# A modulation chunk's gate: products on VectorE in the feed-forward part instead of matmuls in the mixing part

## The chip, the cores and the metric

The kernel runs on one core of one Trainium2 chip. The time is that of one launch in device microseconds; a time is the median of several launches. One more launch was recorded by the profiler.

## The reference, cut to what matters

Two layers on 256 tokens `x` and 256 context tokens `ctx` of width 1024, followed by a second network of two blocks that the change doesn't touch. Each of the two layers computes from one vector `c` (and one `c_ctx` for the context) six chunks of 1024 modulation values; the last chunk, number 5, is the gate of the feed-forward part, and it is used only where that part's result is added.

```python
s_lat, s_ctx = silu(c), silu(c_ctx)
mod   = s_lat @ w_mod[i] + b_mod[i]      # w_mod[i]: 1024 x 6144
mod_c = s_ctx @ w_mod[i] + b_mod[i]
sh1, sc1, g1, sh2, sc2, g2 = split(mod, 6)

def _ffn_sublayer(x, shift, scale, gate, p):
    h = rms_norm(x, p['g_pre_ffn']) * (1 + scale) + shift
    f = square(relu(h @ p['w_ff1'])) @ p['w_ff2']     # 1024 -> 4096 -> 1024
    return x + gate * rms_norm(f, p['g_post_ffn'])
```

## The kernel before

All is float32. Each matmul of the layers is three passes (`mm3`, L212): stationary and moving operand are split in a high and a low part, and high x high, high x low and low x high are added. A weight tile `raw` (512 KB, a ring of 5) is loaded by a DMA that SyncE issues; ScalarE copies it to the high part `wh` (L226), VectorE subtracts for the low part `wl` (L227), 128x512 at a time, ten buffers each. SyncE's queue is in order: a load that waits for a free `raw` holds back all loads behind it.

The modulation values of layer 0 are made in two ways. Chunks 0 and 1 come at the very start. Chunks 2 to 5 are two units of 2048 columns in the mixing part (`mod_units((0, 1), (0, 2))`): for each of eight steps over the 1024 inputs, two `raw` tiles with two column groups each are loaded, and four float32 matmuls of 32 rows x 512 columns (L303), each on its own 32 columns of the array, add into one PSUM tile `fl`. Four transposes (L310) and an addition (L314) end a unit.

The modulation values of layer 1 are made during the feed-forward part of layer 0, by `mod_sums` (L323 to L357): VectorE multiplies a `raw` tile by the token's value and adds it to an accumulator `q` (L340 for the first product, L342 for the others, 128x512 each), a matmul with ones sums over the partitions (L346, one for each accumulator, on 32 columns of the array each, into `fl`), then four transposes and an addition follow. One call of `step()` issues the products of one `raw` tile: four where two token kinds are wanted, two where one is.

The feed-forward part (`ffn`) goes in eight rounds `r_` of 512 hidden features: a first product with w_ff1 (four tiles of features), the square of its positive part (L947 to L950), a second product with w_ff2 that is added to `acc` (L966). In round 0 the first product goes in two halves of 256 columns, that of the tokens `X` and that of the context `CTX`, since the context's input `h2c` is made last (transposes L420, scaling L424 and split L226/L227, from `modulated`). `mod_gate` (L387 to L395) spreads the gate over the partitions: 8 transposes (L393) and two copies into `q` buffers for each token kind; before, this stands at the head of `ffn`, and its four `q` buffers (of eight) stay in use until the end of it.

The order of the instructions on each engine is not that of the source. A scheduler in the build orders them by priority and by its own estimate of when operands are there; on the chip each engine then works through its list in order. Buffers of a ring are handed out in that order, too.

Of the kernel before, what the change touches and what calls it, by code (L numbers as in the profile page):

```python
# [1 line left out]

# [62 lines left out]
def body(ctx, tc, A, out):  # L65
# [44 lines left out]
    def FL():  # L110
        return pfl.tile([P, 512], F32, tag="fl", name=nm("fl"))
# [208 lines left out]
    ones = C([P, 32], "c_ones")  # L320
    POOL.memset(ones, 1.0)

    def mod_sums(i):  # L323

        nrow = A["w_mod"][i].rearrange("(k p) n -> p k n", p=P)
        for kinds, nb, b0 in (((0, 1), 2, 0), ((0, 1), 2, 2), ((0,), 4, 4), ((0,), 4, 8)):
            accs = []
            for b in range(b0, b0 + nb):  # L330
                acc = [Q() for _ in kinds]
                accs += acc
                for k in range(0, KT, 2):
                    r = raw.tile([P, 1024], F32, tag="raw", name=nm("raw")).rearrange("p (k c) -> p k c", k=2)
                    SP.dma_start(r, nrow[:, k:k + 2, 512 * b:512 * b + 512])
                    for q in range(2):
                        for o, a in zip(kinds, acc):
                            w = sT[:, k + q, o:o + 1]
                            if k + q == 0:
                                DVE.tensor_scalar(a, r[:, q, :], w, None, ALU.mult)  # L340
                            else:
                                DVE.scalar_tensor_tensor(a, r[:, q, :], w, a, ALU.mult, ALU.add)  # L342
                    yield
            ps = FL()
            for g, a in enumerate(accs):
                PE.matmul(ps[32 * g:32 * g + 32, :], ones, a, start=True, stop=True, skip_group_check=True)  # L346
            r = R()
            ACT.copy(r, ps)
            for j in range(4):
                PE.transpose(ps[:, j * P:(j + 1) * P], r[:, j * P:(j + 1) * P], ident)  # L350
            nr = len(kinds)
            t4 = ps.rearrange("p (j b r q) -> p b j r q", j=4, b=nb, r=nr)
            for b in range(nb):
                k = 4 * (b0 + b)
                DVE.tensor_tensor(mods[i][:, k:k + 4, 0:nr], t4[:, b, :, :, 0],
                                  cols[i][:, O_BM + k:O_BM + k + 4, None].to_broadcast([P, 4, nr]), ALU.add)
            yield  # L357

    def mod_units(*units):

        def steps():
            for i, u in units:
                yield from mod_steps(i, [2048 * u + 512 * g for g in range(4)], 512, FL())
        return stepping(steps())

    def stepping(it):
# [536 lines left out]
    def ffn(i, h2, h2x, h2c, step, done):  # L903
        last = i == 1
        pairs = (X,) if last else (X, CTX)
        acc = {}
        gate = {r: mod_gate(i, 5, O_GQF, r) for r in ((0,) if last else (0, 1))}
        for r_ in range(8):
            if r_ == 0 and last:

                nb = 2
                Ws = [wblk(A["w_ff1"][i], [(512 * q, 512)], keep=KT if q else 0) for q in range(nb)]
                first = {(t, q): (U(F32R), U(F32R)) for t in range(2) for q in range(nb)}
                for t in range(2):
                    for q in range(nb):
                        ps = AN()
                        mm3(ps, tok(h2x, t, Ws[q]))
                        r, f2 = R(), R()
                        ACT.activation(r, ps, AF.Relu)
                        DVE.tensor_tensor(f2, r, r, ALU.mult)  # L920
                        tp = TP()
                        for ft in range(4):
                            PE.transpose(tp[:, ft * P:(ft + 1) * P], f2[:, ft * P:(ft + 1) * P], ident)
                        split(tp, *first[t, q])
            if last and r_ < nb:
                parts, srcs = (), ()
                fT = None
            else:
                W6 = wblk(A["w_ff1"][i], [(512 * r_, 512)])
                if last:  # L930
                    parts, srcs = ((0, 256),), (h2x,)
                elif r_ == 0:
                    parts, srcs = ((256, 512), (0, 256)), (h2x, h2c)
                else:
                    parts, srcs = ((0, 512),), (h2,)
                if last:
                    q_ = [U(F32R) for _ in range(4)]
                    fT = [(q[:, 0:256], q[:, 256:512]) for q in q_]
                else:
                    fT = [(U(F32R), U(F32R)) for ft in range(4)]  # L940
            for (a, b), src in zip(parts, srcs):
                for ft in range(4):
                    ps = AN()
                    mm3(ps[:, a:b], feat(W6, ft, src, 0, b - a))
                    r, f2 = R(), R()
                    h, l = cut(fT[ft], a, b)
                    ACT.activation(r[:, a:b], ps[:, a:b], AF.Relu)  # L947
                    ACT.activation(h, r[:, a:b], AF.Square)
                    POOL.tensor_tensor(f2[:, a:b], r[:, a:b], r[:, a:b], ALU.mult)  # L949
                    DVE.tensor_tensor(l, f2[:, a:b], f(h), ALU.subtract)  # L950
                    if r_:
                        step(2)
            W7 = [wblk(A["w_ff2"][i], [(512 * n, 512)], 4 * r_, 4) for n in range(2)]
            for pair in (pairs if r_ == 7 else (sum(pairs, ()),)):
                by_token = r_ == 7 and pair == X
                for t, n in [(t, n) for t in pair for n in range(2)] if by_token else [(t, n) for n in range(2) for t in pair]:
                    ps = AN()
                    if fT is None:
                        mm3(ps, [(cut(first[t - 2, r_], k * P, (k + 1) * P), W7[n][k]) for k in range(4)])
                    else:  # L960
                        mm3(ps, tok(fT, t - 2 if last else t, W7[n]))
                    if r_ == 0:
                        acc[t, n] = U()
                        ACT.copy(acc[t, n], ps)
                    else:
                        DVE.tensor_tensor(acc[t, n], acc[t, n], ps, ALU.add)  # L966
                    if r_ == 7 and n == 1:
                        postnorm(t, [acc[t, 0], acc[t, 1]], gate[0 if t >= 2 else 1])
                if r_ == 7:
                    done(pair)  # L970
# [333 lines left out]
    out_projection(0, yT, mid0)  # L1304
    sc1 = C([P, 8, 2], "c_scale1_1")
    POOL.memset(mods[1], 0.0)
    step = stepping(mod_sums(1))
    hT, hc, hx = both()

    def end0(pair):  # L1310
# [24 lines left out]
    def step(n=1):  # L1335
        calls[0] += 1
        if calls[0] == 20:
            first.append(ple(0))
# [31 lines left out]
```

## Time and profile before

| | us |
|---|---|
| median of 3 launches | 1543.09 |
| the three launches | 1543.09, 1537.67, 1543.42 |
| the profiled launch | 1537.98 |
| its span from the first to the last instruction | 1535.9 |
| TensorE (PE) busy in it | 1470.2 |
| VectorE (DVE) busy | 1036.4 |
| ScalarE (ACT) busy | 740.4 |
| GpSimd (POOL) busy | 308.2 |

The mixing part of layer 0 lies at about 55 to 325 us of the span, its feed-forward part at about 325 to 685 us, layer 1 behind it to about 1050 us. Round 0 of the feed-forward part ends on TensorE at 362.87 us. Times of single instructions overlap on TensorE: what one takes of the engine is read from its start to the start of the next.

### The profile page before, as it was taken

The page shows a single profiled execution, that of the slowest core. Times are in us where ns is not written, and L with a number is a line of the kernel's source. Part 1 is how long each engine was busy: PE and PEld are TensorE (multiplying, and loading weights), DVE is VectorE, ACT ScalarE, POOL GpSimd, SP SyncE. Part 2 cuts the span into 40 slices and gives each one's busy share as a digit, 9 for nine tenths or more (in the row PEclk, how much of TensorE's full clock was granted, in tenths as well). Part 3 has the DMA queues.
Part 4 walks back from the last instruction along what each step waited for, and adds up shares of the span by engine and source line. Part 5 has one row for each costly group of instructions (what it writes and reads, how often), then busy time and mean ns, then how long its engine had stood idle before and what let it go on. Part 6 is the DMA issues. An engine that isn't in the chain of part 4 may idle for free.

```text
span 1535.9 us, 23433 instructions
## 1 busy us (share of the span) xinstructions
PE 1470.2 (96%) x8417; PEld 1215.3 (79%) x8417; DVE 1036.4 (67%) x2057; ACT 740.4 (48%) x1594; POOL 308.2 (20%) x356
## 2 busy tenths in 40 slices
PE   6997999999999999998899899999999999999998
PEld 4766678888878888878797689997888889878886
DVE  3559556478597557478776756676876786567866
ACT  3433345564233333255556654565566457445663
POOL 1225201150001111034331301112310320021110
PEclk9998999999999999999999999999999999999999
DMA  9854622325366546334423546555436550645442
GB/s 294 266 182 153 219 84 88 97 66 195 123 219 206 180 152 200 109 83 135 132 76 117 165 139 213 188 195 169 153 107 203 162 179 15 219 139 180 138 149 69
DMA packets 131687, 236.51 MB, mean 154 GB/s; under 512 B 12624, under 2 KB 31251, under 8 KB 131571
## 3 DMA queue, kind: packets, MB, share of 16 engines
q1 hardware_dynamic: 130688, 233.46, 47.0%
q0 software_dynamic: 704, 1.50, 0.3%
q8 instruction: 66, 1.08, 0.3%
q14 instruction: 50, 0.41, 0.1%
q10 hardware_dynamic: 179, 0.06, 0.0%
HBM read 233.87 MB, written 1.11 MB: 153 GB/s over the span
## 4 chain that ended last, share of the span: by engine, by line
PE 84%; DVE 7%; DMA 4%; issue 2%; ACT 2%; POOL 1%; SPq 0%; ACTq 0%; DVEq 0%; POOLq 0%
PE sc L212 47%; PE mm L212 20%; PE tp L459 3%; DVE wl L227 2%; PE fl L303 2%; DMA raw<-in_w_mod_dram 1%; DMA raw<-in_ple_w_gate_dram 1%; PE fl L212 1%; DMA raw<-in_w_in_dram 1%; PE sc L793 1%; PE mm L639 1%; PE sc L1083 1%; PE sc L634 1%; DVE u L782 1%; PE sc L1108 1%
## 5 line engine op out<-in xcount | busy, mean ns | idle before, releaser
L227 DVE TENSOR_TENSOR wl<-raw,wh 128x512 fp32r<-128x512 f32 (+1 forms) x606 | 421.2, 731 | 141.1 <-ACT wh L226 138.1
L226 ACT CAST wh<-raw 128x512 fp32r<-128x512 f32 (+1 forms) x606 | 359.2, 620 | 307.0 <-PE sc L212 104.5
L212 PE MATMUL sc<-wh,u 128*128 128x512 f32 (+2 forms) x1424 | 458.6, 389 | 3.5 <-DVE r L505 2.0
L212 PEld LDWEIGHTS sc<-wh,u 128*128 128x128 f32 x1424 | 265.4, 189 | 58.8 <-ACT p L226 2.2
L212 PE MATMUL sc<-wl,u 128*128 128x512 f32 (+2 forms) x712 | 274.6, 387 | 0.1
L212 PE MATMUL sc<-u,wh 128*128 128x256 f32 (+1 forms) x1072 | 265.1, 336 | 1.8 <-ACT wh L226 1.1
L212 PE MATMUL mm<-wh,u 128*128 128x512 f32 (+1 forms) x648 | 219.3, 395 | 1.0 <-ACT u L226 1.0
L212 PEld LDWEIGHTS sc<-u,wh 128*128 128x128 f32 x1072 | 184.0, 191 | 24.5 <-issue 2.0
L212 PE MATMUL sc<-u,wl 128*128 128x256 f32 (+1 forms) x536 | 178.0, 335 | 0.0
L212 PEld LDWEIGHTS sc<-wl,u 128*128 128x128 f32 x712 | 134.6, 189 | 24.8 <-DVE wl L227 0.5
L949 POOL TENSOR_TENSOR r<-r 128x256 f32<-128x256 f32 (+1 forms) x60 | 64.3, 1073 | 420.1 <-ACT r L947 380.2
L212 PEld LDWEIGHTS mm<-wh,u 128*128 128x128 f32 x648 | 122.2, 190 | 26.1 <-ACT u L226 1.7
L212 PE MATMUL mm<-wl,u 128*128 128x512 f32 (+1 forms) x324 | 127.2, 393 | 0.0
L212 PE MATMUL mm<-u,wh 128*128 128x256 f32 (+1 forms) x512 | 117.6, 317 | 1.1 <-ACT wh L226 1.0
L212 PEld LDWEIGHTS sc<-u,wl 128*128 128x128 f32 x536 | 102.0, 191 | 9.6
L342 DVE SCALAR_TENSOR_TENSOR q<-raw,c_sT,q 128x512 f32<-128x512 f32 x112 | 85.0, 788 | 13.8 <-DMA raw<-in_w_mod_dram 13.2
L212 PEld LDWEIGHTS mm<-u,wh 128*128 128x128 f32 x512 | 86.1, 191 | 9.2 <-issue 1.7
L212 PE MATMUL mm<-u,wl 128*128 128x256 f32 (+1 forms) x256 | 80.4, 314 | 0.0
L950 DVE TENSOR_TENSOR u<-r,u 128x256 fp32r<-128x256 f32 (+1 forms) x60 | 33.6, 561 | 63.0 <-POOL r L949 60.7
L1016 POOL TENSOR_TENSOR r<-r,r 128x512 f32<-128x512 f32 (+1 forms) x30 | 44.6, 1491 | 151.4 <-DVE r L1014 151.3
L212 PEld LDWEIGHTS mm<-wl,u 128*128 128x128 f32 x324 | 61.5, 190 | 12.5 <-issue 0.8
L227 POOL TENSOR_TENSOR u<-r,u 128x256 fp32r<-128x256 f32 (+1 forms) x48 | 38.2, 801 | 119.3 <-ACT u L226 119.0
(318 smaller groups left out, 1984.7 us busy)
## 6 DMA issues: line engine op xcount, KB each, us to landing
raw<-in_w_ff_dram SPq DMA_DIRECT2D x128, 512.0 KB, 4.5
raw<-in_w_mod_dram SPq DMA_DIRECT2D x80, 512.0 KB, 4.5
raw<-in_a_w_in_dram SPq DMA_DIRECT2D x80, 512.0 KB, 3.9
raw<-in_w_in_dram SPq DMA_DIRECT2D x32, 512.0 KB, 5.1
raw<-in_b_w_in_dram SPq DMA_DIRECT2D x18, 512.0 KB, 4.6
raw<-in_w_mod_dram SPq DMA_DIRECT2D x32, 256.0 KB, 5.2
raw<-in_w_out_dram SPq DMA_DIRECT2D x16, 512.0 KB, 3.8
raw<-in_ple_w_gate_dram SPq DMA_DIRECT2D x16, 512.0 KB, 3.9
```

What stands on the lines that cost most here:

```text
L212: PE.matmul(ps, s, m, start=(i == 0), stop=(i == n - 1))
L226: ACT.copy(h, src)
L227: (eng or DVE).tensor_tensor(l, src, f(h), ALU.subtract)
L303: PE.matmul(ps[32 * g:32 * g + 32, :], sT[:, k + q, :], rs[g // per][:, q, w * (g % per):w * (g % per) + w], start=(k + q == 0), stop=(k + ...
L342: DVE.scalar_tensor_tensor(a, r[:, q, :], w, a, ALU.mult, ALU.add)
L459: PE.transpose(tp[:, b * P:(b + 1) * P], p[:, b * P:(b + 1) * P], ident)
L634: PE.matmul(ps[:, b * P:(b + 1) * P], qT[t][:, hs], kT[b][:, hs], start=True, stop=True, skip_group_check=True)
L639: PE.matmul(po[64 * e:64 * e + 64, hp * P:(hp + 1) * P], V[b // 2][:, 256 * (b % 2) + 64 * h:256 * (b % 2) + 64 * h + 64], pT[e][:, b * P: ...
L782: DVE.tensor_scalar(o, o, cs[:, t, c:c + 1], 0.0, ALU.subtract, ALU.min)
L949: POOL.tensor_tensor(f2[:, a:b], r[:, a:b], r[:, a:b], ALU.mult)
L950: DVE.tensor_tensor(l, f2[:, a:b], f(h), ALU.subtract)
L1016: POOL.tensor_tensor(a[:, 0:w], a[:, 0:w], b[:, 0:w], ALU.add)
```

## The change

The second unit of layer 0 shrinks from 2048 to 1024 columns (chunk 4 alone). It keeps its eight steps with four matmuls each, now of 256 columns, and one `raw` tile holds all four groups of a step. Chunk 5 (columns 5120 to 6143) goes to `mod_sums(0, ...)`: two blocks of 512 columns for both token kinds, nine steps, 32 products and four matmuls with ones, chained ahead of layer 1's 52 steps. Round 0 of the feed-forward part, which had no step before, takes one at each of its eight tiles; the other rounds take two, as before. `mod_gate` is called in round 6 of layer 0 behind the loads of w_ff2, and in layer 1 in round 0 behind them. The diff (numbers of lines are those of the kernel before; in the kernel after they are 2 to 6 higher):

```diff
@@ -320,12 +322,12 @@
-    def mod_sums(i):
+    def mod_sums(i, groups):
         nrow = A["w_mod"][i].rearrange("(k p) n -> p k n", p=P)
-        for kinds, nb, b0 in (((0, 1), 2, 0), ((0, 1), 2, 2), ((0,), 4, 4), ((0,), 4, 8)):
+        for kinds, nb, b0 in groups:
             accs = []
@@ -358,9 +360,11 @@
     def mod_units(*units):
         def steps():
             for i, u in units:
-                yield from mod_steps(i, [2048 * u + 512 * g for g in range(4)], 512, FL())
+                w = 512 if u == 1 else 256
+                yield from mod_steps(i, [2048 * u + w * g for g in range(4)], w, FL()[:, 0:w])
         return stepping(steps())
@@ -904,7 +908,6 @@
         last = i == 1
         pairs = (X,) if last else (X, CTX)
         acc = {}
-        gate = {r: mod_gate(i, 5, O_GQF, r) for r in ((0,) if last else (0, 1))}
         for r_ in range(8):
@@ -948,9 +951,10 @@
                     DVE.tensor_tensor(l, f2[:, a:b], f(h), ALU.subtract)
-                    if r_:
-                        step(2)
+                    step(2 if r_ or last else 1)
             W7 = [wblk(A["w_ff2"][i], [(512 * n, 512)], 4 * r_, 4) for n in range(2)]
+            if r_ == (0 if last else 6):
+                gate = {r: mod_gate(i, 5, O_GQF, r) for r in ((0,) if last else (0, 1))}
@@ -1304,7 +1308,9 @@
     POOL.memset(mods[1], 0.0)
-    step = stepping(mod_sums(1))
+    step = stepping(itertools.chain(mod_sums(0, (((0, 1), 2, 10),)),
+                                    mod_sums(1, (((0, 1), 2, 0), ((0, 1), 2, 2), ((0,), 4, 4), ((0,), 4, 8)))))
```

**What moves on the engines.** TensorE in the mixing part, where the second unit's last steps stand among the products of the scan (`sc_1590`, after: `sc_1580`) and of attention (L459, L634). Before:

```order
L806 MATMUL sc_1569<-u_1103,u_778 128x256
L303 MATMUL fl_1446<-raw_1584,c_sT_114 32x512 x2
L765 MATMUL sc_1591<-u_777,u_776 128x128
L765 MATMUL sc_1591<-u_778,u_776 128x128
L303 MATMUL fl_1446<-raw_1626,c_sT_114 32x512 x2
L459 MATMUL tp_1720<-c_ident_104,p_1715 128x128 x4
L303 MATMUL fl_1446<-raw_1628,c_sT_114 32x512 x2
L459 MATMUL tp_1737<-c_ident_104,p_1734 128x128 x4
L303 MATMUL fl_1446<-raw_1634,c_sT_114 32x512 x2
L793 MATMUL sc_1590<-r_1594,u_1598 128x64
L303 MATMUL fl_1446<-raw_1636,c_sT_114 32x512 x2
```

and the same place after:

```order
L769 MATMUL sc_1581<-u_777,u_776 128x128
L769 MATMUL sc_1581<-u_778,u_776 128x128
L463 MATMUL tp_1706<-c_ident_104,p_1701 128x128 x4
L463 MATMUL tp_1723<-c_ident_104,p_1720 128x128 x4
L638 MATMUL mm_1798<-u_1660,q_1728 128x128
L638 MATMUL mm_1798<-u_1711,q_1728 128x128
L797 MATMUL sc_1580<-r_1584,u_1588 128x64
L214 MATMUL sc_1770<-u_149,wh_1732 128x512
L638 MATMUL sc_1813<-u_1660,q_1728 128x128
L638 MATMUL sc_1813<-u_1711,q_1728 128x128
L214 MATMUL sc_1770<-u_150,wh_1732 128x512
```

Before, the second unit has 16 pieces of two matmuls in the whole list (5 in a row, 9 single ones, and 2 much later); after, 8 pieces of four (5 in a row, 2 single ones, and one much later).

VectorE at the same place, up to the row that the scan's matmul (`u_1598`, after: `u_1588`) waits for. Before:

```order
L808 TENSOR_TENSOR r_1562<-sc_1563,u_916 128x512
L782 TENSOR_SCALAR u_1608<-u_1608,c_cs_621 128x128 x4
L592 COPY u_618<-mm_1711 128x256
L808 TENSOR_TENSOR r_1568<-sc_1569,u_916 128x512
L787 TENSOR_TENSOR s_1605<-sc_1591,c_tri_573 128x128
L787 TENSOR_TENSOR s_1615<-sc_1591,c_tri_573 128x128
L787 TENSOR_TENSOR s_2140<-sc_1591,c_tri_573 128x128
L787 TENSOR_TENSOR s_2150<-sc_1591,c_tri_573 128x128
L788 TENSOR_TENSOR u_1598<-u_1598,s_1605 128x512
```

and after:

```order
L812 TENSOR_TENSOR r_1556<-sc_1557,u_916 128x512
L229 TENSOR_TENSOR wl_1757<-raw_1750,wh_1756 128x512
L812 TENSOR_TENSOR r_1562<-sc_1563,u_916 128x512
L596 COPY u_618<-mm_1697 128x256
L229 TENSOR_TENSOR wl_1763<-raw_1760,wh_1762 128x512
L791 TENSOR_TENSOR s_1595<-sc_1581,c_tri_573 128x128
L791 TENSOR_TENSOR s_1605<-sc_1581,c_tri_573 128x128
L791 TENSOR_TENSOR s_2126<-sc_1581,c_tri_573 128x128
L791 TENSOR_TENSOR s_2136<-sc_1581,c_tri_573 128x128
L229 TENSOR_TENSOR wl_1767<-raw_1760,wh_1766 128x512
L229 TENSOR_TENSOR wl_2164<-raw_2161,wh_2163 128x512
L792 TENSOR_TENSOR u_1588<-u_1588,s_1595 128x512
```

Nine weight splits (five of them above this piece) that stood behind that row stand ahead of it now.

VectorE at the start of the feed-forward part, from the end of the context's normalisation (L410, after: L414) on; the rows L424 (after: L428) make `h2c`. Before:

```order
L387 TENSOR_TENSOR s_3176<-c_mod_122,c_cols_137 128x8
L387 TENSOR_TENSOR s_3192<-c_mod_122,c_cols_137 128x8
L410 TENSOR_SCALAR q_3098<-u_2690,s_3091 128x512
L410 TENSOR_SCALAR q_3099<-u_2691,s_3091 128x512
L424 TENSOR_SCALAR r_3105<-tp_3102,c_scale_4623_2612,c_mod_122 128x256
L424 TENSOR_SCALAR r_3112<-tp_3109,c_scale_4623_2612,c_mod_122 128x256
L424 TENSOR_SCALAR r_3119<-tp_3116,c_scale_4623_2612,c_mod_122 128x256
L227 TENSOR_TENSOR u_2597<-r_3105,u_2596 128x256
L424 TENSOR_SCALAR r_3126<-tp_3123,c_scale_4623_2612,c_mod_122 128x256
L424 TENSOR_SCALAR r_3133<-tp_3130,c_scale_4623_2612,c_mod_122 128x256
```

and after, behind the last L414:

```order
L342 TENSOR_SCALAR q_3237<-raw_3239,c_sT_114 128x512
L342 TENSOR_SCALAR q_3238<-raw_3239,c_sT_114 128x512
L342 TENSOR_SCALAR q_3387<-raw_3389,c_sT_114 128x512
L342 TENSOR_SCALAR q_3388<-raw_3389,c_sT_114 128x512
L428 TENSOR_SCALAR r_3087<-tp_3084,c_scale_4615_2594,c_mod_122 128x256
L428 TENSOR_SCALAR r_3094<-tp_3091,c_scale_4615_2594,c_mod_122 128x256
L344 SCALAR_TENSOR_TENSOR q_3237<-raw_3239,c_sT_114,q_3237 128x512
L344 SCALAR_TENSOR_TENSOR q_3238<-raw_3239,c_sT_114,q_3238 128x512
L344 SCALAR_TENSOR_TENSOR q_3387<-raw_3389,c_sT_114,q_3387 128x512
L344 SCALAR_TENSOR_TENSOR q_3388<-raw_3389,c_sT_114,q_3388 128x512
L428 TENSOR_SCALAR r_3101<-tp_3098,c_scale_4615_2594,c_mod_122 128x256
L229 TENSOR_TENSOR u_2579<-r_3087,u_2578 128x256
```

It goes on in this way: between the last L414 and the last VectorE row that writes a part of `h2c` stand 33 rows now, 20 of them products of chunk 5. On SyncE the eight loads of chunk 5 stand between round 0's loads of w_ff1 and those of w_ff2.

## Rows read from the trace of the kernel before

**Rows 1.** Page, part 1: busy time (share of the span) and instructions.
```profile
PE 1470.2 (96%) x8417; PEld 1215.3 (79%) x8417; DVE 1036.4 (67%) x2057; ACT 740.4 (48%) x1594; POOL 308.2 (20%) x356
```

**Rows 2.** Busy time of each engine by window, then clock, DMA share, GB/s.
```profile
140.00:160.00 20.00, 18.37 (x116) 11.52 (x115) 14.07 (x38) 6.03 (x14) 8.50 (x12) 1.00 0.77 263
...
360.00:380.00 20.00, 20.00 (x90) 16.58 (x89) 17.41 (x25) 6.58 (x12) 2.71 (x2) 1.00 0.68 229
```

**Rows 3.** Timeline of PE, mixing part: start, duration, engine, line, form, count.
```profile
143.96 2.77 PE L303 MATMUL fl<-raw,c_sT 128*32 128x512 f32 x20
...
149.65 1.05 PE L303 MATMUL fl<-raw,c_sT 128*32 128x512 f32 x4
150.63 1.10 PE L793 MATMUL sc<-r,u 128*128 128x64 f32 x8
...
166.06 0.43 PE L793 MATMUL sc<-r,u 128*128 128x64 f32 x2
```

**Rows 4.** Timeline of DVE, mixing part.
```profile
152.68 0.56 DVE L227 TENSOR_TENSOR p<-tp,p 128x384 fp32r<-128x384 f32 x1 [1.39 <-ACT p L226]
...
157.23 3.52 DVE L782 TENSOR_SCALAR u<-u,c_cs 128x128 f32<-128x128 f32 x4
...
163.44 1.25 DVE L788 TENSOR_TENSOR u<-u,s 128x512 f32<-128x512 f32 x1
```

**Rows 5.** Timeline of DVE, start of the feed-forward part.
```profile
323.44 0.99 DVE L424 TENSOR_SCALAR r<-tp,c_scale,c_mod 128x256 f32<-128x256 f32 x2
...
330.13 0.53 DVE L424 TENSOR_SCALAR r<-tp,c_scale,c_mod 128x256 f32<-128x256 f32 x1
...
340.18 0.42 DVE L950 TENSOR_TENSOR u<-r,u 128x256 fp32r<-128x256 f32 x1
340.51 4.29 DVE L227 TENSOR_TENSOR wl<-raw,wh 128x512 fp32r<-128x512 f32 x7
...
349.20 0.88 DVE L340 TENSOR_SCALAR q<-raw,c_sT 128x512 f32<-128x512 f32 x2 [3.47 <-DMA raw<-in_w_mod_dram]
350.00 3.40 DVE L342 SCALAR_TENSOR_TENSOR q<-raw,c_sT,q 128x512 f32<-128x512 f32 x5
```

**Rows 6.** Timeline of PE, round 0's two products and the gate's transposes.
```profile
332.72 1.03 PE L393 MATMUL tp<-c_ident,s 128*128 128x128 f32 x8
333.51 0.36 PE L212 MATMUL mm<-u,wh 128*128 128x256 f32 x1
...
340.73 0.40 PE L212 MATMUL sc<-u,wh 128*128 128x256 f32 x2
340.96 0.28 PE L212 MATMUL sc<-u,wl 128*128 128x256 f32 x1
341.08 0.40 PE L212 MATMUL sc<-wh,u 128*128 128x512 f32 x1
...
362.87 0.62 PE L212 MATMUL sc<-u,wh 128*128 128x512 f32 x2
```

**Rows 7.** Timeline of PE: matmuls with ones, four together and one alone.
```profile
411.93 1.06 PE L346 MATMUL fl<-q,c_ones 128*32 128x512 f32 x8
...
440.55 1.04 PE L346 MATMUL fl<-q,c_ones 128*32 128x512 f32 x2
441.53 0.50 PE L212 MATMUL sc<-wh,u 128*128 128x512 f32 x1
```

**Rows 8.** Timeline of POOL and of DVE at one moment.
```profile
370.67 1.04 POOL L949 TENSOR_TENSOR r<-r 128x512 f32<-128x512 f32 x1 [25.40 <-ACT r L947]
...
370.71 1.55 DVE L227 TENSOR_TENSOR wl<-raw,wh 128x512 fp32r<-128x512 f32 x1
```

**Rows 9.** Page, part 6: one load: count, KB, us from issue to landing.
```profile
raw<-in_w_mod_dram SPq DMA_DIRECT2D x80, 512.0 KB, 4.5
```

**Rows 10.** PE's busy time, then granted clock, in windows of 2 us.
```profile
322.00:324.00 2.00, 0.44 (x2) 1.00 0.00 0
...
326.00:328.00 2.00, 1.98 (x9) 0.50 0.00 0
```

More of the change, by code (lines that the diff above doesn't have):

```diff
@@ L1 @@
+import itertools
 import numpy as np
```

## The prediction

> **What bounds the kernel now.** I read the busy times first: TensorE works 1470 of 1535.9 us, VectorE 1036 [rows 1]. A change can gain by taking work from TensorE, or lose by making it wait; VectorE's average leaves room, so the question is where it has none. Windows tell that [rows 2]: in the mixing part at 140 to 160 us TensorE is busy 18.37 of 20 us and VectorE 14.07, and in round 0 and 1 of the feed-forward part (360 to 380) TensorE is busy without a gap and VectorE 17.41. The change takes matmuls out of the first place and puts 32 products, in VectorE's order, at the head of the second, where the same list also has to make the context's input `h2c`. The timelines of these two places give every term below.
>
> **Term 1, the second unit on TensorE.** Alone, a piece of two matmuls (four records) takes from 149.65 to 150.63, 0.98 us; five pieces in a row take 2.77 less the overlap, 2.7 us [rows 3]. The unit has 5 in a row and 11 single ones: 2.7 + 11 x 0.98 = 13.5 us. After, a piece is four matmuls of half the columns. Four matmuls on four column groups take as long as one, 1.06 against 1.04 us [rows 7], so I let the groups run side by side and halve the columns: 0.5 us in a row, 0.55 alone, 5 x 0.5 + 3 x 0.55 = 4.15 us. Gain in TensorE's work: 9.3 us (5.7 us if a piece of half the columns takes 0.98 all the same).
>
> **What of it reaches the end.** The change also brings the next weights in earlier (eight fewer 512 KB loads stand before them), and with them nine weight splits move ahead of the row of VectorE (L788, ends at 164.69 [rows 4]) for which the scan's matmul waits that TensorE started at 166.06 [rows 3]. Count VectorE anew from there: the first of these splits needs the third of five loads issued at some 144 to 147 us; a load lands in 4.5 us alone [rows 9], and five share the way, so I take 152 and 0.6 for ScalarE's copy. From 152.6 on: 9 splits at 0.61 (seven in 4.29 [rows 5]) = 5.5; the split of `p`, 0.5; three additions and products at 0.6, 1.8; a copy, 0.35; four L782, 0.9 to 3.5 [rows 4], I take 2.1; four L787 and the L788, 1.7. Sum 12.0: the row ends at 164.6, as before (164.69). TensorE, 7 us earlier with its own work by then, waits and starts that matmul at 164.6 and not at 166.06: 1.5 us gained. Behind it there were three more pieces of the unit (2.9 us), now one (0.55): 2.4 us. **Term 1 is -3.9 us.** Bounds: -9.3 if VectorE never delays TensorE; -1 if L782 takes its 3.5 us and the loads come late (row at 167).
>
> **Term 2, round 0.** Before, the last context row ends at 330.66 (330.13 + 0.53), 7.2 us behind the last L410, since little else stands there [rows 5]. After, 33 rows stand between, and with the last one itself it is 34: 4 first products at 0.44 (two in 0.88), 16 further products at 0.68 (five in 3.40), 8 L424 at 0.47, 6 short subtractions at 0.42 [rows 5]: 1.8 + 10.9 + 3.8 + 2.5 = 19.0 us. I add no wait for their data: five of the eight loads find a free buffer ahead of this place, and the sixth, which goes out when the first buffer is free again (327.5), lands at 332.0 [rows 9], as the row that reads it comes up (332.2). So `h2c` is complete at 323.4 + 19.0 = 342.4, 12 us later than before. GpSimd works in the same stretch, and a two-operand row of VectorE beside it takes 1.55 us where seven in a row take 0.61 each [rows 8, 5]; eight GpSimd rows of some 0.75 us fall into it, so 0 to 6 us more, of which I take 3: 345.4.
>
> The Trainium skill (GPSIMD Engine Reference, "1. Specifications") says that GpSimd shares its SBUF interface with VectorE, with contention for instructions with two SBUF inputs. The chunk's products are of that kind, so the rule speaks against this place for them, and the rows on the slowed split agree with it. By the rule alone each of the eight GpSimd rows would cost its time, 6 us and not 3, and the sum below would be 3 us higher.
>
> TensorE meanwhile runs out of work. It needs the fifth of eight parts of `h2c` with 84 matmuls of 256 columns to go (0.12 us each, two in 0.23 [rows 6]) and the seventh with 20 to go. The fifth is there after 12.6 of the 19.0 us (4 first products, 10 further ones, 6 L424, 3 subtractions), at 336 without GpSimd's share and 338 with it: 338 + 84 x 0.12 = 348.1; by the seventh 345.4 + 2.4 = 347.8. Both say that the first product ends at 348, not 341.08 [rows 6]. The second product takes 362.87 - 341.08 = 21.8 us as before, plus the four matmuls with ones, which stand there one by one at 1.0 us each [rows 7]: 25.8. Round 0 ends at 373.8 where it ended at 362.87: **term 2 is +10.9 us.** The loads of w_ff2 wait on SyncE behind the chunk's eight, which wait for buffers that the products free; the first goes out at some 338 and the last at 347, each lands 4.5 us later [rows 9], and VectorE comes to their splits later than that (345 to 357), so I add nothing for them. Bounds: +8 (no share for GpSimd, one of the ones under a wait: 346.2 + 24.8 = 371.0) to +15 (VectorE, slowed by 6 us, also late with the last splits of w_ff2: 376; and 1.7 us for the clock: after the gap at 322 to 324 TensorE had half its clock, 0.50, at 326 to 328, 1.2 and not 2.4 GHz [rows 10]; the gap would be three times as long now).
>
> From round 1 on VectorE is ahead again: its rows up to the next w_ff1 end at about 370, and TensorE comes at 373.8. I add nothing; its cover is some 4 us, and what is lost beyond that is TensorE's.
>
> **Term 3, the small ones.** The 16 transposes of the gates stood inside round 0's first product (8 in 0.79 [rows 6], 16 in some 1.5); they move to round 6, where TensorE is as full: +1.5, since term 2 counts to round 0's end without them. Layer 1's sixteen matmuls with ones stand in pieces of 1, 1+1+2, 1, 1+3 now and of 1+3, 1+3, 1, 1 then ("1" for four together): seven pieces of 1.0 against six, -1.0. One more set of transposes for the chunk, one set half as long: +0.2. In layer 1 the gate's 8 transposes leave a place beside waits for one that is full, 0 to +0.8; I take +0.3. **Sum +1.0.** The accumulators gain: the gate no longer holds four of eight `q` buffers, so a group need not wait for the ones of the one before; VectorE gains, TensorE doesn't wait for that.
>
> **Sum.** -3.9 + 10.9 + 1.0 = +8.0 us. Against the profiled launch, 1537.98, that is 1546.0. Two of the four launches shown lie near 1538 and two near 1543, the median (1543.09) with the upper ones; against the mean of the four, 1540.5, it is **1548.5 us**.
>
> **Rivals.** (a) TensorE's work decides, not VectorE's order: the products fill idle time of VectorE, as the scheduler meant, and both waits vanish under other matmuls. Then -9.3 in the mixing part, +4.0 for the ones, +1.0: -4.3 us, 1536; with the four ones under gaps of TensorE too, -8.3, 1532. For it: VectorE is idle a third of the time [rows 1], and before, `h2c` was complete at 330.7 while TensorE had use for it until 341 [rows 5, 6]. Against it: TensorE's list after has all four context tiles end behind the seventh part. It decides if `h2c` is complete by some 338. (b) GpSimd and the clock: VectorE's row by row slowdown is met by nearly each of the eight GpSimd rows, the splits of w_ff2 come late as well, and TensorE comes out of two gaps at 1.2 GHz. Then term 2 is +15, term 1 no better than -1 to -2: +14, 1552 to 1557. For it: rows 8 and 10; against it: half of the GpSimd rows fell beside short rows before. (c) Round 0 as forecast, but the mixing part gains all of its 9.3: +2.6, 1543.
>
> **How the numbers follow.** Forecast 0.55, (a) 0.17, (b) 0.16, (c) 0.12. What a measurement can tell here is about 0.5%, 7.7 us. The forecast's own range (+2 to +12) lies half beyond that, 0.30 slower and 0.25 within; (a) halves into 0.09 faster and 0.08 within; (b) is slower, (c) within. Together faster 0.09, within 0.45, slower 0.46. The range leaves out 0.1 below and 0.1 above: from -4 against 1540.5 to +15 against 1543.09, 1536 to 1558.
>
> **What would show it.** Right: in the trace of the changed kernel the pieces of the second unit take about 0.55 us; a scan matmul behind it waits for VectorE; the first product of round 0 shows 5 to 9 us of waiting for rows of `h2c`, with the clock at 0.50 for some of it; four ones of about 1.0 us stand singly in round 0; rounds 1 to 7 show no waits. Wrong: TensorE busy without a gap from 325 to 365, or pieces of 1 us as before, or new waits in rounds 1 to 3, where VectorE has some 45 us of rows for TensorE's 43.5.

## The result, and the profile after

The changed kernel takes 1551.93 us (median of 6), the kernel before 1540.03 (median of 6 in the same comparison): 1.0081 times as long, 95% interval 1.0066 to 1.0097, 12 us slower. The forecast was 1548.5, slower, within 1536 to 1558. The sign and the range held. Of the terms, the one for the mixing part had the wrong sign.

The first line of the page of the kernel after, beside [rows 1]:

```profile
PE 1470.9 (95%) x8427; PEld 1221.1 (79%) x8427; DVE 1053.6 (68%) x2091; ACT 740.9 (48%) x1595; POOL 311.6 (20%) x356
```

The unit's 32 matmuls are half as long now, and yet TensorE's busy time didn't fall: the four matmuls with ones came in, and more of its work ran at half clock (the mean granted clock of the profiled launch is 0.978, before it was 0.986).

Where the time went is read by following one and the same matmul through the traces: its start after, less its start before. A number that grows between two such marks is time lost between them. The marks are at these places of the trace before: 90.17 us (ahead of the change), 220.02 (behind the second unit, in the mixing part), 319.97 (the last matmul ahead of the wait for the context's normalisation), 341.08 (end of round 0's first product), 362.87 (end of round 0), and the end of the span, 1535.9.

| kernel | 90.17 | 220.02 | 319.97 | 341.08 | 362.87 | end |
|---|---|---|---|---|---|---|
| after | 0.99 | 3.35 | 3.57 | 11.21 | 15.79 | 13.47 |
| e1, no step in round 0 | 2.77 | 3.89 | 3.72 | 2.81 | 2.81 | 1.43 |
| e2, whole unit | 3.39 | 3.53 | 3.64 | 11.93 | 14.85 | 17.19 |
| e3, gate alone | 1.89 | 1.80 | 1.82 | 0.47 | 0.47 | -1.48 |
| e4, scan's priority 100 | 5.70 | 2.16 | 6.30 | 14.91 | 17.68 | 18.21 |
| e5, half of the steps | 0.59 | 3.39 | 5.24 | 8.84 | 8.61 | 2.70 |
| e6, gate in other buffers | 2.98 | 3.33 | 3.33 | 3.96 | 3.96 | 2.13 |
| e7, ones by four | 2.68 | 4.31 | 4.13 | 3.79 | 3.79 | 7.24 |
| e8, mask ahead | 2.70 | 1.61 | 1.43 | -0.21 | -0.21 | 0.37 |
| e9, filler | 1.06 | 2.57 | 2.47 | 20.56 | 19.17 | 18.29 |
| e10, scan's priority 0 | 1.59 | 9.23 | 11.78 | 8.93 | 8.93 | 9.74 |

The first column is no effect of an edit: TensorE's instructions are the same up to there in all kernels, and what differs is mostly how fast the first loads came in (TensorE waits 7.9 us for the first `raw` in the trace before, 9.2 in e4's). It scatters from 0.6 to 5.7 us, so each stretch is judged by the difference of two columns, and whole kernels by the medians.

The mixing part, TensorE's timeline (start, duration, engine, line, form, count, and in brackets the wait ahead), beside [rows 3]:

```profile
145.39 2.37 PE L305 MATMUL fl<-raw,c_sT 128*32 128x256 f32 x40
147.69 0.66 PE L463 MATMUL tp<-c_ident,p 128*128 128x128 f32 x4
...
150.68 0.64 PE L305 MATMUL fl<-raw,c_sT 128*32 128x256 f32 x8
151.25 0.66 PE L797 MATMUL sc<-r,u 128*128 128x64 f32 x4
...
161.87 0.63 PE L463 MATMUL tp<-c_ident,p 128*128 128x128 f32 x4 [2.30 <-ACT p L622]
163.78 0.80 PE L638 MATMUL mm<-u,q 128*128 128x128 f32 x4 [1.28 <-ACT q L465]
168.17 0.66 PE L797 MATMUL sc<-r,u 128*128 128x64 f32 x2 [3.59 <-DVE u L792]
168.59 0.77 PE L214 MATMUL sc<-u,wh 128*128 128x512 f32 x1
```

Five pieces of the unit in a row take 147.69 - 145.39 = 2.3 us, a single one 0.57. So the unit did shrink, to some 4 us. But the scan's late matmul starts at 168.17 and not at 166.06, behind a wait of 3.59 us. The two waits for ScalarE ahead of it (2.30 and 1.28 us) are over before that row of VectorE is, so the row decides when TensorE goes on. VectorE's rows and GpSimd's ahead of it, beside [rows 4]:

```profile
146.94 0.68 DVE L792 TENSOR_TENSOR u<-u,s 128x512 f32<-128x512 f32 x1
...
153.65 1.67 DVE L229 TENSOR_TENSOR wl<-raw,wh 128x512 fp32r<-128x512 f32 x2 [0.92 <-ACT wh L228]
...
156.43 1.34 DVE L229 TENSOR_TENSOR wl<-raw,wh 128x512 fp32r<-128x512 f32 x1 [0.65 <-ACT wh L228]
...
158.29 1.28 DVE L229 TENSOR_TENSOR wl<-raw,wh 128x512 fp32r<-128x512 f32 x2
...
163.96 2.40 DVE L229 TENSOR_TENSOR wl<-raw,wh 128x512 fp32r<-128x512 f32 x2
166.28 1.74 DVE L792 TENSOR_TENSOR u<-u,s 128x512 f32<-128x512 f32 x1
...
164.11 1.70 POOL L813 TENSOR_TENSOR q<-q,r 128x512 f32<-128x512 f32 x1
165.77 1.71 POOL L792 TENSOR_TENSOR u<-u,s 128x512 f32<-128x512 f32 x1
```

Two weight splits that take 1.28 us together at 158.29 take 2.40 beside a row of GpSimd, and the row that is waited for takes 1.74 beside another, where a row of the same line and size took 0.68 at 146.94.

TensorE's busy time and granted clock in windows of 2 us, mixing part and round 0, beside [rows 10]:

```profile
166.00:168.00 2.00, 0.00 (x0) 0.50 0.78 241
168.00:170.00 2.00, 1.83 (x8) 0.50 0.17 31
172.00:174.00 2.00, 2.00 (x6) 0.50 0.63 241
...
326.00:328.00 2.00, 0.44 (x2) 1.00 0.00 0
330.00:332.00 2.00, 0.45 (x3) 0.50 0.03 7
342.00:344.00 2.00, 2.00 (x12) 0.50 0.52 182
346.00:348.00 2.00, 2.00 (x19) 1.00 0.01 4
```

The clock is at 0.50 (1.2 GHz) from within the wait until some 174.3 us, where before it was at 1.00 throughout 160 to 180 us. In round 0 it is low from about 328 to 345 us, in the last 5 us of it with TensorE busy all the time.

Round 0, VectorE's timeline, beside [rows 5]:

```profile
326.12 0.88 DVE L414 TENSOR_SCALAR q<-u,s 128x512 f32<-128x512 f32 x2 [0.84 <-POOL s L170]
326.92 1.67 DVE L342 TENSOR_SCALAR q<-raw,c_sT 128x512 f32<-128x512 f32 x4
...
329.41 2.73 DVE L344 SCALAR_TENSOR_TENSOR q<-raw,c_sT,q 128x512 f32<-128x512 f32 x4
...
343.36 0.53 DVE L428 TENSOR_SCALAR r<-tp,c_scale,c_mod 128x256 f32<-128x256 f32 x1
...
346.71 0.41 DVE L229 TENSOR_TENSOR u<-r,u 128x256 fp32r<-128x256 f32 x1
```

From the end of the last L414 (327.0) to the end of the last L428 (343.89) it takes 16.9 us; before it was 7.25 [rows 5]. TensorE's waits of the stretch from 100 to 400 us that belong to these two places (total, times, longest), and the matmuls with ones, beside [rows 7]:

```profile
PE sc L797 <- DVE u L792: 6.9, 3, 3.6
PE tp L424 <- DVE r L428: 5.7, 3, 2.2
```

```profile
358.76 1.04 PE L348 MATMUL fl<-q,c_ones 128*32 128x512 f32 x2
362.69 1.04 PE L348 MATMUL fl<-q,c_ones 128*32 128x512 f32 x2
365.70 1.04 PE L348 MATMUL fl<-q,c_ones 128*32 128x512 f32 x2
367.57 1.04 PE L348 MATMUL fl<-q,c_ones 128*32 128x512 f32 x2
```

### The profile page after: what moved, and what is told of

It reads as the page before. It is cut to its first block, busy times and chain, and to the rows that moved or that the text cites. A ratio compares the mean times of both kernels' runs of the same rounds, so it can differ in the third digit from the quotient of the medians.

```text
span 1549.4 us, 23490 instructions
## 1 busy us (share of the span) xinstructions
PE 1470.9 (95%) x8427; PEld 1221.1 (79%) x8427; DVE 1053.6 (68%) x2091; ACT 740.9 (48%) x1595; POOL 311.6 (20%) x356
## 4 chain that ended last, share of the span: by engine, by line
PE 81%; DVE 9%; DMA 5%; issue 2%; ACT 2%; POOL 1%; SPq 0%; ACTq 0%; DVEq 0%; POOLq 0%
PE sc L214 46%; PE mm L214 20%; PE tp L463 3%; DVE wl L229 2%; DMA raw<-in_w_mod_dram 2%; DMA raw<-in_ple_w_gate_dram 1%; PE fl L214 1%; PE fl L305 1%; DMA raw<-in_w_in_dram 1%; DVE u L786 1%; PE sc L1087 1%; PE mm L643 1%; PE sc L797 1%; PE sc L638 1%; PE tp L424 1%
## 5 line engine op out<-in xcount | busy, mean ns | idle before, releaser
L214 PE MATMUL sc<-u,wh 128*128 128x256 f32 (+1 forms) x1072 | 269.4, 339 | 2.0 <-ACT wh L228 1.0
L214 PEld LDWEIGHTS sc<-u,wh 128*128 128x128 f32 x1072 | 186.7, 193 | 25.3 <-ACT wh L228 1.9
L344 DVE SCALAR_TENSOR_TENSOR q<-raw,c_sT,q 128x512 f32<-128x512 f32 x140 | 105.3, 781 | 15.9 <-DMA raw<-in_w_mod_dram 15.2
```

The costliest lines, as they stand in the source:

```text
L214: PE.matmul(ps, s, m, start=(i == 0), stop=(i == n - 1))
```

## The experiments

The theory after this reading: round 0 loses because the products stand ahead of the rows that make `h2c`; the mixing part loses because the weight splits stand ahead of the row L792. Rival causes: a gap and a low clock that would be there anyway, too little work for TensorE, and, for the second layer, the gate's place.

**e1. No step in round 0.**

```diff
-                    step(2 if r_ or last else 1)
+                    step(2 if r_ or last else 0)
```

> The changed kernel, but round 0 of the first layer's feed-forward part takes no step: chunk 5's products begin in round 1. Theory (the 20 products ahead of the rows that make the context's input cause the loss): that input is complete some 7 us behind the last L414, as in the kernel before, and not 17; round 0's first product loses nothing, its second product has no matmuls with ones (4 us less), rounds 1 to 7 stay without waits and take 2 us for the ones in two pieces. Against the changed kernel's 1552: -7.6 - 4.6 + 2 = -10 us, 1540 to 1543. Rival (TensorE's gap at 324 to 329 us and the low clock behind it come from the normalisation and remain, the products only fill the time): less than 5 us gained, 1547 or more.

Measured: 1539.85 us, 0.9999 times the kernel before (0.9984 to 1.0014). By one number in the source, all that the change lost is back; the 1.1 us that the mixing part still loses here are made up for behind it. VectorE's timeline of the same place:

```profile
326.23 0.88 DVE L414 TENSOR_SCALAR q<-u,s 128x512 f32<-128x512 f32 x2 [0.84 <-POOL s L170]
327.14 1.00 DVE L428 TENSOR_SCALAR r<-tp,c_scale,c_mod 128x256 f32<-128x256 f32 x2
...
333.96 0.55 DVE L428 TENSOR_SCALAR r<-tp,c_scale,c_mod 128x256 f32<-128x256 f32 x1 [0.81 <-PE tp L424]
```

`h2c` is through L428 at 334.51, 7.4 us behind the last L414 (327.11), and round 0 gains 0.9 us on the kernel before (3.72 to 2.81). Here VectorE waits for TensorE, not the other way round. The theory holds. The rival falls: TensorE's gap at 324 to 327 us and a clock of 0.50 at 328 to 334 us are there in this kernel too, and the loss isn't.

**e5. Half of the steps.** Does the loss follow the number of products?

```diff
-                    step(2 if r_ or last else 1)
+                    step(2 if r_ or last else int(a == 0))
```

> The changed kernel, but round 0 takes a step only at the four tiles of the context: 10 of chunk 5's products stand ahead of the last row of the context's input and not 20, and the matmuls with ones come four together in five places (none in round 0). Theory (each product ahead delays the context's input by its own time): the input is complete some 12 us behind the last L414, where it was 17; round 0's first product loses about 4 us and not 7.6; without the ones round 0's second product loses nothing (-4.6), and the ones cost 5 x 1.0 later, about 2 us less than in the kernel before in the same stretch. 1552 - 3.8 - 4.6 - 1 = 1542 to 1544. Rival (TensorE falls to half clock whatever the length of the wait, and pays most of the 7.6): 1546 or more. Rival (half the products are hidden as they were meant to be): 1538 to 1539.

Measured: 1544.18 us, 1.0017 (1.0006 to 1.0028).

```profile
328.07 0.88 DVE L414 TENSOR_SCALAR q<-u,s 128x512 f32<-128x512 f32 x2 [0.84 <-POOL s L170]
328.87 0.87 DVE L342 TENSOR_SCALAR q<-raw,c_sT 128x512 f32<-128x512 f32 x2
...
336.19 1.40 DVE L344 SCALAR_TENSOR_TENSOR q<-raw,c_sT,q 128x512 f32<-128x512 f32 x2
...
340.11 0.98 DVE L428 TENSOR_SCALAR r<-tp,c_scale,c_mod 128x256 f32<-128x256 f32 x2
```

The three kernels side by side, counted from the end of the last L414:

| products ahead of the last L428 | last L428 ends after | first product ends after |
|---|---|---|
| 0 (e1) | 7.4 us | 16.8 us |
| 10 (e5) | 12.1 us | 21.0 us |
| 18 (after; 20 ahead of the last split) | 16.9 us | 25.3 us |

Both columns rise by a straight line: 0.47 to 0.53 us of VectorE's time for a product, and TensorE pays 4.2 of 4.7 and 8.5 of 9.5 us. So the loss follows the length of the delay, and both rivals of this run fall: its first product loses 3.6 us by the marks, not 7.6 and not nothing. The three kernels don't part the delay from the clock, though: it is at 0.50 for some 7 us in e1, 10 in e5 and 17 in the changed kernel, so it grows with the products as well.

**e2. The mixing part undone.**

```diff
-                w = 512 if u == 1 else 256
+                w = 512
```

> The changed kernel, but the second unit is computed in full again (2048 columns, chunk 5 too, with its eight loads and its matmuls), while chunk 5 comes from VectorE's products in round 0 as well and overwrites it: only the mixing part is undone. Theory (from the trace after: the mixing part lost some 2.4 us although TensorE has 9 us less work there): 2 to 3 us faster than the changed kernel, 1549 to 1550. Rival (the prediction's term, a gain of 3.9 us there): 4 us slower, 1556.

Measured: 1553.63 us, 1.0077 (1.0053 to 1.0101): by the time alone no different from the changed kernel, so the medians decide for neither. The marks do for the mixing part: from 90.17 to 220.02 us this kernel loses 0.1 us, as e3 and e6 do, which have the old mixing part too (-0.1, 0.35), while the five kernels with the changed one lose 2.4 (after), 1.1 (e1), 2.8 (e5), 1.6 (e7) and 1.5 (e9). The shrunk unit costs 1 to 3 us there. What e2 wins so it loses behind round 0, where it adds 2.3 us and the changed kernel wins 2.3 back. 2.7 us of that arise between 700 and 800 us of the trace before, in the second layer's mixing part. There the code and the order on TensorE, VectorE, ScalarE and GpSimd are the same in both, and yet e2 has a low clock where the changed kernel hasn't. Windows of TensorE, e2 first:

```profile
730.00:740.00 10.00, 8.35 (x42) 0.66 0.18 54
```

```profile
730.00:740.00 10.00, 7.99 (x62) 1.00 0.20 54
```

Why the clock fell in the one and not in the other stays open.

**e4. The scan ahead of the splits.**

```diff
-        @steps_sooner(0 if last else -300)
+        @steps_sooner(0 if last else 100)
         def scans():
```

> The changed kernel with the scan's priority raised (100 in place of -300), so that the row L792 which the scan's late matmul waits for stands ahead of the nine weight splits again on VectorE. Theory (these splits hold that row back, and TensorE waits for it and then runs at half clock): the waits at 160 to 168 us go, the mixing part gains 4 to 8 us, 1544 to 1548. Rival (TensorE lacks work there whatever VectorE's order is): waits of the same size elsewhere in the mixing part, 1551 to 1553.

Measured: 1550.31 us, 1.0069 (1.0048 to 1.0091). Up to 220.02 us this kernel gains 3.5 us where the changed one loses 2.4: with no split ahead of the row, the mixing part does win, 5.9 us more than the changed kernel. The edit moves the whole scan, on TensorE too, so the row isn't shown to be the only reason. Then 4.1 us go again up to 319.97: at 311.76 TensorE waits 1.97 us for the rows that make the tokens' input, a wait that the kernel after doesn't have, and runs at half clock until some 315.7. The theory holds for the place and falls for the sum, TensorE's timeline:

```profile
309.19 0.60 PE L424 MATMUL tp<-c_ident,q 128*128 128x128 f32 x4
311.76 0.92 PE L424 MATMUL tp<-c_ident,q 128*128 128x128 f32 x4 [1.97 <-DVE r L428]
```

**e8. Only the masking rows ahead,** on top of e1.

```diff
-                        DVE.tensor_tensor(pm, pc[...], tri[...], ALU.mult)
-                        (POOL if d == 1 and not last else DVE).tensor_tensor(heads(row, P), ...)
+                        with tc.high_priority(offset=0 if last else 300):
+                            DVE.tensor_tensor(pm, pc[...], tri[...], ALU.mult)
+                            (POOL if d == 1 and not last else DVE).tensor_tensor(heads(row, P), ...)
```

> As the run without steps in round 0, but the scan's masking rows (L791 and L792 alone) have a higher priority, so that six weight splits and not nine stand ahead of the row that the scan's late matmul waits for. Theory (three splits, some 2 us, are the wait): TensorE's wait there falls from 3.6 to about 1.6 us, with less time at half clock behind it, 1537 to 1539. Rival (what is gained there is lost again at the end of the mixing part, where TensorE waits for the normalisation): 1540.

Measured: 1536.67 us, 0.9971 (0.9957 to 0.9986): faster than both kernels. Up to 220.02 us it gains 1.1 us where e1 loses 1.1. TensorE's timeline there:

```profile
163.39 2.97 PE L214 MATMUL mm<-u,p 128*128 128x512 f32 x9
166.26 0.63 PE L463 MATMUL tp<-c_ident,p 128*128 128x128 f32 x4
167.69 0.63 PE L463 MATMUL tp<-c_ident,p 128*128 128x128 f32 x4 [0.80 <-ACT p L622]
168.86 0.41 PE L798 MATMUL sc<-r,u 128*128 128x64 f32 x2 [0.54 <-DVE u L793]
169.07 0.71 PE L214 MATMUL sc<-u,wh 128*128 128x512 f32 x2
```

The row still ends at 168.7 us, some 1 us earlier than in the kernel after once the late start is taken off (2.70 against 0.99). More of the gain is TensorE's own order, which differs from e1's from 137 us on: nine matmuls of 2.97 us fall into the wait, which shrinks to 0.54 us, and two matmuls behind it take 0.71 us where they took 1.05 in the kernel after (at 170.87). The time came as expected, only in part by the way that the expectation named.

**e10. The scan at priority 0,** on top of e1.

```diff
-        @steps_sooner(0 if last else -300)
+        @steps_sooner(0 if last else 0)
         def scans():
```

> As the run without steps in round 0, but with the scan's priority at 0 in place of -300: four weight splits and not nine stand ahead of the row that the scan's late matmul waits for, and the scan's matmuls stand earlier among those of attention on TensorE. Theory (the fewer splits ahead of that row, the less of the mixing part is lost): 3 us or more faster than the run without steps (1540), 1534 to 1537. Rival (what the scan gains is lost at the end of the mixing part, as in the run with priority 100): 1539 to 1541.

Measured: 1546.75 us, 1.0037 (1.0022 to 1.0052). Both expectations miss: this order loses 7.6 us up to 220.02 already, with clocks of 0.66, 0.69 and 0.50 in the windows of 10 us from 120 to 150 us (0.81, 0.66 and 1.00 in the kernel before). The number of splits ahead of one row is no measure of an order; where else TensorE waits counts as much.

**e3. The gate's later place alone,** in the kernel before.

```diff
-        gate = {r: mod_gate(i, 5, O_GQF, r) for r in ((0,) if last else (0, 1))}
         for r_ in range(8):
...
             W7 = [wblk(A["w_ff2"][i], [(512 * n, 512)], 4 * r_, 4) for n in range(2)]
+            if r_ == (0 if last else 6):
+                gate = {r: mod_gate(i, 5, O_GQF, r) for r in ((0,) if last else (0, 1))}
```

> The kernel before with one part of the change alone: the gate is made in round 6 in the first layer and behind round 0's loads of w_ff2 in the second. Theory (16 transposes leave round 0 and come back in round 6, TensorE is full in both): the same time within 1.5 us, with round 0 ending 1.5 us earlier. Rival (the 3.5 us that the changed kernel wins back in the second layer come from the gate's later place): 3 to 4 us faster than the kernel before.

**e6. The gate in other buffers,** in the kernel before, its place unchanged.

```diff
-            o = Q()
+            o = U() if i == 0 and chunk == 5 else Q()
```

> The kernel before with one thing changed: the gate of the first layer's feed-forward part is written to four buffers of the ring u instead of four of the eight q; its transposes stay at the beginning of that part. Theory (what the gate's later place gains is that products no longer wait for q buffers, in the kernel before 9.6 us of VectorE's waiting for the matmuls with ones, so these come in fewer pieces): as in the run of the gate alone, 2 to 3 us faster than the kernel before, 1538. Rival (the gain is from the transposes, which left round 0): the time of the kernel before, within 1 us.

Measured: e3 1538.10 us, 0.9983 (0.9969 to 0.9998); e6 1538.33, 0.9981 (0.9967 to 0.9995). By the medians both are some 2.5 us faster than the kernel before. e6 leaves the transposes where they were, so this gain needs the four `q` buffers alone. VectorE's waits from 340 to 640 us show the buffers, in the kernel before:

```profile
DVE q L340 <- PE fl L346: 9.6, 2, 5.7
```

Twice a first product waits until matmuls with ones have freed an accumulator. No such wait is left in e3, e6 or the kernel after, and layer 1's ones stand in six places, not seven. Behind round 0, e3 gains 2.0 us by the marks and e6 1.8. Only part of that lies in the feed-forward part: at 700.71 us of the trace before, behind its last matmuls with ones, e6 has gained 1.2 us since the end of round 0 (3.96 to 2.77) and e3 nothing (0.47 to 0.54), where its 16 transposes come in again. A piece of ones fewer is worth 1.0 us of this [rows 7]. The rest arises in the second layer, where the clock scatters as in e2, and isn't shown to be the buffers'.

**e7. The ones four together,** on top of e1.

```diff
-                    step(2 if r_ or last else 1)
+                    step((3 if ft % 2 else 2) if r_ or last else 0)
```

> As the run without steps in round 0, but with 3 and 2 steps by turns at the tiles of the later rounds in place of 2: by the order of the instructions the matmuls with ones then come four together in all five places, not in eight pieces. Theory (a piece costs TensorE 1.0 us whether it holds one or four): 3 us faster than that run, 1537. Rival (the pieces cost nothing, or VectorE, with a quarter more products in each round, comes late for rounds 1 to 3): 1540 or more, with waits for rows of VectorE in these rounds.

Measured: 1542.07 us, 1.0005 (0.999 to 1.002). Not faster than e1, but not for the rival's reason either: from 366 to 640 us TensorE waits for nothing. At 640 us of the trace before, e7 stands 0.6 us behind round 0's end (3.79 to 4.38) and e1 3.3 us (2.81 to 6.12), so the ones in fewer pieces did save 2.7 us (3.0 at 700.71, behind the last of them). Behind the feed-forward part they are lost; the windows with a low clock in the second layer are longer in e7 (below, at 770 us; in e1 there it is 0.83). Which of its waits brings that about isn't settled.

```profile
770.00:780.00 10.00, 7.86 (x37) 0.66 0.28 78
```

**e9. Filler for TensorE,** in the changed kernel.

```diff
+            if idle:
+                for _ in range(idle):
+                    PE.transpose(tp[:, 256:384], ident, ident)
...
-        modulated(normed(pair), ...)
+        modulated(normed(pair), ..., idle=0 if pair == X else 6)
```

> The changed kernel with 48 more transposes of a constant on TensorE, six behind each of the eight pieces of the context's input, whose result nobody reads: they stand in the places of round 0 where TensorE waits for VectorE. Each takes 0.11 us at full clock, 0.21 at half. Theory (part of the loss is TensorE's half clock from 329 to 345 us, some 2.5 us in the stretch from 339.6 to 345.2 in which it has work and no wait): the granted clock stays nearer to 1.00 there and the kernel gains 1 to 3 us, 1549 to 1551. Rival (the context's input, complete at 344 and split at 346, sets the end whatever the clock is, and the filler only takes time): 1552 to 1556.

Measured: 1556.74 us, 1.0105 (1.0081 to 1.0128), slower. The clock rose to 1.00 at 334 to 338 us and fell again (0.50 at 342 to 344). VectorE's rows changed their order as well: the last L428 stands at 349.94, behind 26 products and two weight splits and not behind 18 products. So this kernel changes more than the filler, and it doesn't show what the low clock alone costs in round 0.

## Why the prediction was right or wrong

| term | forecast | by the marks |
|---|---|---|
| mixing part (90.17 to 319.97) | -3.9 | +2.6 |
| round 0, first product (to 341.08) | +6.9 | +7.6 |
| round 0, second product (to 362.87) | +4.0 | +4.6 |
| the small ones (to the end) | +1.0 | -2.3 |
| ahead of the change (to 90.17) | 0 | +1.0 |
| sum, profiled launches | +8.0 | +13.5 |

The range held in part by luck. The mixing part came out 6.5 us worse than forecast, round 0 and the first 90 us 2.3 us worse, the rest 3.3 us better; the medians, 12 us apart, lie between the forecast and the marks.

**Round 0 was right in mechanism; in its size two errors offset each other.** The 33 rows ahead of the last split and that one took from 327.0 to 347.12, 20.1 us, where 19.0 and 3 for GpSimd had been forecast. The share of GpSimd is seen in the later pairs of products: 1.87, 1.89, 1.76 and 1.76 us beside rows of GpSimd, 1.40 alone (e5 at 336.19), 1.7 us in all. So the fifth part of `h2c`, taken for 338, was there at 339.49, or 335.9 without the 3.6 us by which this kernel was late already: 2 us sooner than forecast. The 84 matmuls behind it, taken for 0.12 us each or 10.1 in all, ran without a gap from 339.55 to 352.30, 12.75 us, since the clock was at 0.50 for the first 26. The sum had no term for that, only the upper bound had (1.7 us); it cost some 2.6 us here. TensorE's timeline where they begin:

```profile
339.21 0.69 PE L424 MATMUL tp<-c_ident,q 128*128 128x128 f32 x2 [1.48 <-DVE r L428]
339.55 0.57 PE L214 MATMUL sc<-u,wh 128*128 128x256 f32 x1
```

The Trainium skill (GPSIMD Engine Reference, "1. Specifications") says that GpSimd and VectorE share an SBUF interface and contend for it. The trace agrees in kind, with 1.7 us; the section gives no size, and the prediction's estimate from it, each of GpSimd's rows at its full time, would have been 6 us.

The four ones stand singly at 1.04 us, as forecast. The 16 transposes that left the first product (1.5 us) are in its +7.6; e3 shows them alone, -1.35.

**Term 1 had the wrong sign, and the step that failed is the wait for the row ahead of the scan's matmul, and what follows it.** The unit's own size was right (4.15 us forecast, 4.0 measured). The row was to end at 164.6; it ended at 168.0, 167.0 without the late start, where the bound for the worst case stood. That is 2.4 us late. The loads weren't the reason: [rows 9] is the median of 80 loads and not one load alone, but the first split came as reckoned (153.65, or 152.7 without the late start). The sum of rows on VectorE took GpSimd's contention into account in round 0 alone, though the same [rows 8] applied here: one split at 156.43 took 1.34 instead of 0.68, two 2.40 instead of 1.28, the row itself 1.74 instead of 0.68, 2.8 us in all. A wait of 0.65 for ScalarE comes on top, and four L786 took 0.86 instead of the 2.1 put down for them. The second omission is the clock: behind the wait TensorE ran at 0.50 until 174.3, three matmuls in 1.28 us (170.44 to 171.72) instead of 0.69, about 3 us. A wait of TensorE was priced by its length, and not by what TensorE does after it. Three waits of 0.5 us each at 188 to 192 us, where the kernel before has one of 0.4, are the last piece. Together that is some 6.5 us, the whole miss. That the unit's matmuls had kept TensorE busy through this place was seen, but counted as cost only.

**Term 3 isn't refuted by its sign.** The -2.3 us are of one trace. From the end of round 0 to 700.71 us the changed kernel loses 1.6 us (15.79 to 17.41), where the terms for the feed-forward part come to +0.7. What it wins back behind that, 3.9 us, arises in the second layer, where e2 with the same code wins nothing (17.01 to 17.19). The sentence that TensorE doesn't wait for the accumulators isn't refuted either: e6 wins 1.2 us in the feed-forward part, and 1.0 of it is the piece of ones that the forecast had counted. By its median e6 wins some 2.5 us; where the rest comes from stays open. The ones and their places came as forecast.

**The rivals.** (a), that VectorE has room, falls: e1 and e5 show that each product ahead of `h2c` is paid for. (b) came nearest in time (1552 to 1557), and its two mechanisms, GpSimd's contention and the clock, did act. In the mixing part they did more than the 2 to 3 us over the forecast that it allowed; round 0 stayed at +12.2, under its +15. (c) falls with term 1. The forecast's other signs were right: ones alone in round 0, waits for rows of `h2c` with the clock at 0.50, and 0.4 us of waiting in rounds 1 to 7.

## What to carry to other kernels

Work that goes to an engine with a low average must be costed at the place in its list where it lands: here 18 to 20 rows of 0.5 us each, ahead of rows that TensorE waits for, cost nearly their full time, and the same rows one round later made TensorE wait for 0.2 us. Work taken from TensorE gains only where nothing else ends late there; ask first which matmul stands behind it and what that one waits for. And a buffer held across a phase can cost as much as the work that fills it: some 2.5 us by e6's median, against 1.5 for the 16 transposes.

## What the runs showed of the hardware

- A row of VectorE with two large operands beside one of GpSimd took up to 2.6 times its time (1.74 us at 166.28, 0.68 at 146.94).
- After a stretch with hardly any matmuls the clock stayed at 0.50 for some 5 us in which TensorE was busy without a gap (340 to 345 us), and the same instructions of the second layer, in the same order, ran at 0.66 in one kernel and at 1.00 in another (730 to 740 us). A difference of 2 to 4 us that arises there in one trace can't be put down to an edit.
- The first 90 us vary by 5 us from one profile to the next, though TensorE has the same instructions there.
